# U products moved behind each head's routing, gathers begun there, and one-hot rows by pairs of tokens, in a two-block decoder kernel

## The chip, the cores and the metric

One core of one Trainium2 chip runs the whole program. The metric is device microseconds of one execution, compared as the median of several. The names are those of the profile: PE (matrix engine, with PEld for its weight loads), DVE (vector engine), ACT (scalar engine), POOL (GpSimd), SP (the queue that issues most DMAs).

## The reference, cut to what matters

The program is two decoder blocks on 512 tokens of width 1024. The change touches only its last layer, a product-key expert layer ("PEER"), which for 512 tokens, 8 heads, 2 x 128 keys and 16384 experts computes:

```
q = (h @ w_q).reshape(B, S, 8, 256)
s1 = einsum('bshd,hnd->bshn', q[..., :128], keys1);  s2 = ... keys2
v1, i1 = top_k(s1, 16);  v2, i2 = top_k(s2, 16)
cand = v1[..., :, None] + v2[..., None, :]
vals, c = top_k(cand.reshape(..., 256), 16)
expert = e1 * 128 + e2
gate = softmax(vals)
act = gelu(einsum('td,ted->te', h, u_tab[expert]))
out = x + einsum('te,ted->td', gate * act, v_tab[expert])
```

Each token thus has 8 x 16 = 128 experts; each has a row u and a row v of 1024 numbers.

## The kernel before, in words

The first some 1626 us are the rest of the network and are not touched. `peer` (L1354) then works in three stages.

**Routing.** For each of 8 heads `proj_tr` multiplies h by that head's part of w_q (48 matmuls of 512 columns; every product of this kernel is three matmuls of split fp32 halves, `mm3`), `route` (L1540) scores the keys (16 small matmuls) and finds the top 16 of 128 twice and of 64 candidates once by MAX8, FIND_INDEX8 and MATCH_REPLACE8 on DVE, then turns them into expert numbers by one-hot sums on DVE. Tiles of this stage come from the pool `p_rt` with two buffers. The softmax over all heads stands once behind the loop (L1385 to L1392), as does the number of each expert of the last 128 tokens, `ei` (L1394).

**Gates.** The first 384 tokens (DT = 3 blocks of 128) are computed densely: all 16384 experts for every token, with a gate matrix that is mostly zero. `gates` (L1500) builds that matrix, four tokens at a time, 96 times: DVE writes one-hot rows `ehot` (L1525) and their product with the gate's three bf16 parts, `p` (L1528); PE makes four 128 x 128 blocks from them with 12 matmuls (L1533); ACT copies the bank into a tile of 16 tokens (L1535), which goes to DRAM (`Gd`, L1538). Four tokens lie side by side in the last dimension of `ehot` and `p`, so each matmul reads every fourth bf16 element.

**Experts.** Experts go in 128 groups of 128. `up(e)` (L1423) loads 512 KB of U through `load_w` (ACT writes the high part, DVE subtracts for the low part, L194 and L195; three buffers each), makes 24 matmuls of 384 columns (name A) and applies Gelu. Group e's result is then multiplied by its gates (L1471), split, and multiplied by 512 KB of V: 18 matmuls of 512 columns (name acc), accumulated in six PSUM banks over all 128 groups. 42 groups (AHEAD) are made before the first V product, 12 of them spilled to DRAM; the other 86 go one per V product. The last 128 tokens are not dense: `gather(j)` (L1410) fetches for each of the 128 expert slots one row of u and v per token by an indirect DMA of POOL (1 MB), DVE makes the dot product (L1415) and adds the weighted v row into x (L1419), ACT does the Gelu between (L1417, L1418). They are spread over the V products.

**What sets the order.** Each engine runs its own instructions in the order that a list scheduler wrote at build time. The scheduler takes what its own model of the times holds to be ready, in program order where several are. `tc.high_priority` and `tc.issue_after(i)` move that order: the second keeps an instruction behind i on i's engine. A tile of a pool waits until the buffer that it takes is free.

Of the kernel before, what the change touches and what calls it, by code (L numbers as in the profile page):

```python
# [7 lines left out]
F32 = mybir.dt.float32  # L8
F32R = mybir.dt.float32r
BF = mybir.dt.bfloat16  # L10
# [7 lines left out]
NT = 4  # L18
DT = 3
TG = 16  # L20
# [162 lines left out]
class Prog:  # L183
# [5 lines left out]
    def split(s, h, l, src, eng="act"):  # L189
        nc = s.nc  # L190
        if eng == "dve":
            r = nc.vector.tensor_copy(h, src)
        else:
            r = nc.scalar.activation(h, src, AF.Copy)  # L194
        s.sub = (nc.gpsimd if eng == "pool" else nc.vector).tensor_tensor(l, src, h.bitcast(F32), ALU.subtract)  # L195
        return r
# [1157 lines left out]
    def peer(s, Y):  # L1354
# [4 lines left out]
        with ExitStack() as ctx:  # L1359
            P = lambda name, bufs, **k: ctx.enter_context(tc.tile_pool(reuse_waits="tile", name=name, bufs=bufs, **k))  # L1360
            one, two, gp = P("p_one", 1), P("p_two", 2), P("p_g", 2)
# [4 lines left out]
            nc.sync.dma_start(s.iota, a["cf"][:, 392:])  # L1366
            s.iota4 = one.tile([128, 128, 4], BF, name="iota4")
            nc.vector.tensor_copy(s.iota4, s.iota[:, :, None].to_broadcast([128, 128, 4]))

            s.E = one.tile([128, NT, 2, 128], F32, name="E")  # L1370
            s.gate = one.tile([128, NT, 8, 16], F32, name="gate")
            with tc.tile_pool(reuse_waits="tile", name="p_rt", bufs=2) as rt:
                s.rank = rt.tile([128, 16, 16 * NT], BF, name="rank", bufs=1)
# [9 lines left out]

                g = s.gate.rearrange("p i h r -> p (i h) r")
                n = 8 * NT  # L1385
                sm = rt.tile([128, n], F32, name="sm")
                nc.vector.tensor_copy(sm, g[:, :, 0])
                nc.vector.tensor_tensor(g, g, sm[:, :, None].to_broadcast([128, n, 16]), ALU.subtract)
                nc.scalar.activation(g, g, AF.Exp)
                nc.vector.tensor_reduce(sm, g, AX.X, ALU.add)  # L1390
                nc.vector.reciprocal(sm, sm)
                nc.vector.tensor_tensor(g, g, sm[:, :, None].to_broadcast([128, n, 16]), ALU.mult)  # L1392
            ei = one.tile([128, 128], I32, name="ei")
            nc.vector.scalar_tensor_tensor(ei, s.E[:, DT, 0], 128.0, s.E[:, DT, 1], op0=ALU.mult, op1=ALU.add)  # L1394
            s.Gd = s.dram.tile([NG, 128, 128, TG], F32, name="Gd")
            with tc.tile_pool(reuse_waits="tile", name="p_hot", bufs=2) as hp:
                s.gates(hp, gp)

            rows = P("p_rows", 3)
            act = two.tile([128, 128], F32, name="act")  # L1400
            wt = two.tile([128, 128], F32, name="wt")
            late = P("p_late", 1)
            x = late.tile([128, 1024], F32, name="x")
            nc.sync.dma_start(x, s.x2[:, DT, :])
            hx = late.tile([128, 1024], F32, name="hx")
            nc.sync.dma_start(hx, s.h2)
            eg = late.tile([128, 128], I32, name="eg")
            gx = s.gate[:, DT].rearrange("p h r -> p (h r)")

            def gather(j):  # L1410
                r = rows.tile([128, 2048], F32, name="r")
                nc.gpsimd.indirect_dma_start(out=r, out_offset=None, in_=a["uv"],  # L1412
                                             in_offset=bass.IndirectOffsetOnAxis(ap=eg[:, j:j + 1], axis=0))
                c = slice(j, j + 1)
                nc.vector.scalar_tensor_tensor(r[:, :1024], r[:, :1024], 1.0, hx,  # L1415
                                               op0=ALU.mult, op1=ALU.mult, accum_out=act[:, c])
                nc.scalar.activation(wt[:, c], act[:, c], AF.Gelu)  # L1417
                nc.scalar.activation(wt[:, c], wt[:, c], AF.Copy, scale=gx[:, c])  # L1418
                nc.vector.scalar_tensor_tensor(x, r[:, 1024:], wt[:, c], x, op0=ALU.mult, op1=ALU.add)  # L1419
            acc = None  # L1420
            wd = s.dram.tile([len(SPILL), 128, ND], F32, name="wd")

            def up(e):  # L1423
                with tc.high_priority(offset=U_AHEAD) if e < 6 else nullcontext():
                    U = s.load_w(a["ut"][e], 1024)
                A = s.bank("A")[:, :ND]
                for k in range(8):
                    s.mm3(A, U(128 * k, 128), (Y[0][:, k, :ND], Y[1][:, k, :ND]), k == 0, k == 7)
                if e in SPILL:
                    w = two.tile([128, ND], F32, name="ws", bufs=2)  # L1430
                else:
                    w = two.tile([128, ND], F32, name="w", bufs=UP + 1)
                    wq[e] = w
                nc.scalar.activation(w, A, AF.Gelu)
                if e in SPILL:
                    nc.sync.dma_start(wd[SPILL.index(e)], w)
            wq = {}
            ahead = AHEAD
            for e in range(ahead):
                up(e)  # L1440

            room, n = [0], ahead
            for e in range(128):
                both = e not in SPILL and n < 128
                room.append(room[-1] + (9 if both else 0 if e in SPILL else 4))
                n += both
            pace = [max(0, min(128, int(128 * (r / room[-1] - .05) / .9))) for r in room]

            gs, subs, m = {}, [], NG // 8

            def fetch(e):
                b, i = e // 8, e % 8
                if i == 0:
                    gs[b] = gp.tile([128, NG, 8, TG], F32, name="g", tag="g")
                i *= m
                nc.sync.dma_start(gs[b][:, i:i + m], s.Gd[i:i + m, :, 8 * b:8 * b + 8, :].rearrange("g p e t -> p g e t"))
            for e in range(8):
                fetch(e)
            for e in range(128):
# [3 lines left out]
                if e in SPILL:  # L1463
                    wq[e] = two.tile([128, ND], F32, name="ws", bufs=2)
# [4 lines left out]
                w3 = w.rearrange("p (g t) -> p g t", t=TG)  # L1469
                with tc.issue_after(subs[e - 2].ins) if e > 1 else nullcontext():  # L1470
# [3 lines left out]
                last = s.split(wh, wl, w)  # L1474
                subs.append(s.sub)
                V = s.load_w(a["uv"][128 * e:128 * e + 128, 1024:], 1024)
                if acc is None:
                    acc = [[s.bank("acc") for n in range(2)] for i in range(DT)]
# [21 lines left out]
    def gates(s, two, gp):  # L1500
# [3 lines left out]
        for i in range(DT):  # L1504
# [4 lines left out]
            T = two.tile([128, 5, 128], BF, name="T", bufs=DT)  # L1509
            nc.scalar.activation(T[:, :3], b[:, :384].rearrange("p (k t) -> p k t", k=3), AF.Copy)  # L1510
# [117 lines left out]
```

## Time and profile before

| | us |
|---|---|
| median of 3 runs (3015.78 to 3022.39) | 3018.95 |
| profiled execution, whole | 3021.56 |
| its span, first to last instruction | 3019.8 |

All times inside the profile are counted from the start of the span. An engine is busy while it has an instruction; matmuls overlap, so the pace of PE is read from the starts of successive matmuls and not from their durations. [...]

### The profile page before, as it was taken

How to read it: one execution, taken by the hardware profiler on the slowest of the kernel's cores; microseconds unless marked ns; L12 is line 12 of the kernel's file. 1: busy time of each engine (PE TensorE's matmuls, PEld its weight loads, DVE VectorE, ACT ScalarE, POOL GpSimd, SP SyncE). 2: the span in 40 equal slices, each digit the busy share in tenths (PEclk: the TensorE clock that was granted, in tenths of full speed). 3: DMA queues.
4: the chain of work that ended last, by engine and by line, in shares of the span. 5: the costliest groups of instructions: out<-in, count | busy, mean ns of one | idle time of the engine just before them, and what ended most of it. 6: DMA issues, size and time to landing. Idle time of an engine off the chain costs nothing. (4 is left out here: it accounts for less than half of the span.)

```text
span 3019.8 us, 44411 instructions
## 1 busy us (share of the span) xinstructions
PE 2901.3 (96%) x17102; PEld 2602.8 (86%) x17103; DVE 2012.7 (67%) x3633; ACT 1340.5 (44%) x2383; POOL 607.4 (20%) x587
## 2 busy tenths in 40 slices
PE   8999999999899999999999799997999999999998
PEld 7877878888789999999988599997888889988977
DVE  5986445553566676765345997775667788787875
ACT  5244433332455565656423345554334344444432
POOL 3001010000455555452200000000111222222210
PEclk9999999999999999999999899998999999999999
DMA  5321132223345555454763134445788899988985
GB/s 194 98 71 63 57 98 98 97 92 98 109 143 161 150 159 161 137 168 141 228 228 127 53 107 143 169 175 180 244 301 307 297 323 337 334 328 299 332 279 198
DMA packets 200149, 549.62 MB, mean 182 GB/s; under 512 B 17360, under 2 KB 90704, under 8 KB 179072
## 3 DMA queue, kind: packets, MB, share of 16 engines
q1 hardware_dynamic: 149184, 358.34, 36.0%
q0 software_dynamic: 49600, 184.76, 17.5%
q10 hardware_dynamic: 1152, 3.67, 0.4%
q8 instruction: 134, 2.20, 0.3%
q14 instruction: 79, 0.65, 0.1%
HBM read 476.52 MB, written 70.19 MB: 181 GB/s over the span
## 5 line engine op out<-in xcount | busy, mean ns | idle before, releaser
L195 DVE TENSOR_TENSOR wl<-wraw,wh 128x1024 fp32r<-128x1024 f32 x474 | 590.3, 1246 | 305.3 <-ACT wh L194 303.4
L194 ACT ACTIVATE wh<-wraw 128x1024 fp32r<-128x1024 f32 (+1 forms) x495 | 520.8, 1054 | 581.6 <-PE bank L201 126.7
L1412 POOL DMA_INDIRECT r<-in_uv_dram,eg x128 | 175.6, 1372 | 1162.7 <-ACT eg L1486 945.9
L202 PE MATMUL A<-yh,wl 128*128 128x384 f32 x1024 | 346.3, 338 | 7.5 <-DVE wl L195 7.4
L200 PE MATMUL A<-yh,wh 128*128 128x384 f32 x1024 | 345.6, 338 | 3.9 <-ACT wh L194 3.3
L201 PE MATMUL A<-yl,wh 128*128 128x384 f32 x1024 | 344.6, 336 | 0.0
L200 PE MATMUL acc<-wh 128*128 128x512 f32 x768 | 304.1, 399 | 19.4 <-ACT wh L194 19.4
L201 PE MATMUL acc<-wl,wh 128*128 128x512 f32 x768 | 305.5, 398 | 0.9 <-DVE wl L195 0.9
L202 PE MATMUL acc<-wh,wl 128*128 128x512 f32 x768 | 292.6, 397 | 3.8 <-DVE wl L195 3.8
L1415 DVE SCALAR_TENSOR_TENSOR r<-r,hx 128x1024 f32<-128x1024 f32 x128 | 156.3, 1221 | 110.1 <-DMA r<-in_uv_dram,eg 108.7
L200 PE MATMUL p<-yh,wh 128*128 128x256 f32 x736 | 214.1, 291 | 7.0 <-DVE l L195 3.8
L202 PE MATMUL p<-yh,wl 128*128 128x256 f32 x736 | 215.7, 293 | 1.4 <-DVE wl L195 1.4
L201 PE MATMUL p<-yl,wh 128*128 128x256 f32 x736 | 213.4, 290 | 0.0
L202 PEld LDWEIGHTS A<-yh,wl 128*128 128x128 f32 x1024 | 192.9, 188 | 10.6 <-DVE wl L195 10.5
L200 PEld LDWEIGHTS A<-yh,wh 128*128 128x128 f32 x1024 | 193.2, 189 | 8.5 <-ACT wh L194 4.2
L201 PEld LDWEIGHTS A<-yl,wh 128*128 128x128 f32 x1024 | 193.1, 189 | 3.7
L200 PEld LDWEIGHTS acc<-wh 128*128 128x128 f32 x768 | 146.2, 190 | 51.0 <-ACT wh L194 20.8
L201 PE MATMUL bank<-yl,wh 128*128 128x512 f32 (+1 forms) x480 | 184.1, 384 | 0.3 <-DMA yl<-od 0.3
L202 PE MATMUL bank<-yh,wl 128*128 128x512 f32 (+1 forms) x480 | 183.5, 383 | 0.0
L200 PE MATMUL bank<-yh,wh 128*128 128x512 f32 (+1 forms) x480 | 182.8, 383 | 0.1
L202 PEld LDWEIGHTS acc<-wh,wl 128*128 128x128 f32 x768 | 145.2, 189 | 39.0 <-DVE wl L195 5.1
L201 PEld LDWEIGHTS acc<-wl,wh 128*128 128x128 f32 x768 | 146.4, 191 | 33.6 <-DVE wl L195 3.2
(576 smaller groups left out, 6914.8 us busy)
## 6 DMA issues: line engine op xcount, KB each, us to landing
wraw<-in_ut_dram SPq DMA_DIRECT2D x128, 512.0 KB, 4.7
wraw<-in_uv_dram SPq DMA_DIRECT2D x128, 512.0 KB, 6.2
Gd<-g SPq DMA_DIRECT2D x24, 1024.0 KB, 4.4
g<-Gd SPq DMA_DIRECT2D x128, 192.0 KB, 7.6
wraw<-in_w_up_dram SPq DMA_DIRECT2D x44, 512.0 KB, 3.7
wraw<-in_w_sb_dram SPq DMA_DIRECT2D x24, 512.0 KB, 4.3
wraw<-in_w_down_dram SPq DMA_DIRECT2D x22, 512.0 KB, 3.8
wraw<-in_w_out_dram SPq DMA_DIRECT2D x16, 512.0 KB, 3.8
```

Source lines behind the costliest of these rows:

```text
L194: r = nc.scalar.activation(h, src, AF.Copy)
L195: s.sub = (nc.gpsimd if eng == "pool" else nc.vector).tensor_tensor(l, src, h.bitcast(F32), ALU.subtract)
L200: nc.tensor.matmul(out, lhsT=L[0], rhs=R[0], start=start, stop=False)
L201: nc.tensor.matmul(out, lhsT=L[0], rhs=R[1], start=False, stop=False)
L202: nc.tensor.matmul(out, lhsT=L[1], rhs=R[0], start=False, stop=stop)
L1412: nc.gpsimd.indirect_dma_start(out=r, out_offset=None, in_=a["uv"], in_offset=bass.IndirectOffsetOnAxis(ap=eg[:, j:j + 1], axis=0))
L1415: nc.vector.scalar_tensor_tensor(r[:, :1024], r[:, :1024], 1.0, hx, op0=ALU.mult, op1=ALU.mult, accum_out=act[:, c])
```

## The change

- Of the 128 U products 64 (instead of 42) now come before the first V product. Six stand behind the routing of each head, eleven behind the gates, and the last five (DRAIN) are kept on DVE behind the last instruction of the gates. 28 of the 64 results stay in SBUF (28 buffers instead of 31) and 36 are spilled to DRAM and fetched again (before: 12 of 42), through three buffers instead of two.
- The softmax and the expert numbers of the gathers are made inside `route`, head by head, so that 21 of the 128 gathers stand among the U products of the routing, 16 among those of the gates and 91 among the V products. A gather, its dot product and its addition are three steps apart: at step e the rows fetched at e-3 are added, those fetched at e-2 are dotted, and new ones are fetched; the DVE and ACT parts are kept behind the weight split of that step. The copies of expert numbers (L1486) go away; the loads of x and hx move up to the first head.
- `route` uses one buffer per tile instead of two; `ehot` and `p` have three buffers instead of five; the gates' 16-token tile now comes from the pool of the gathered rows, which has four buffers (before: three for gathers alone).
- One-hot rows are laid out by pairs: two tokens side by side instead of four, so each matmul reads every second bf16 element. Counts and sizes of the instructions stay.

```diff
-UP = 30
-SPILL = range(6, 42, 3)
-AHEAD = UP + len(SPILL)
+TG = 16
+
+
+AHEAD, UP, UPS, DRAIN = 64, 28, 6, 5
+SPILL = [e for e in range(AHEAD) if e > 1 and e not in {AHEAD * k // (UP - 1) for k in range(UP - 1)}]
...
-            one, two, gp = P("p_one", 1), P("p_two", 2), P("p_g", 2)
+            one, two, rows = P("p_one", 1), P("p_two", 2), P("p_rows", 4)
...
-            with tc.tile_pool(reuse_waits="tile", name="p_rt", bufs=2) as rt:
...
-                nc.vector.tensor_copy(sm, g[:, :, 0])
-                nc.vector.tensor_tensor(g, g, sm[:, :, None].to_broadcast([128, n, 16]), ALU.subtract)
-                nc.scalar.activation(g, g, AF.Exp)
-                nc.vector.tensor_reduce(sm, g, AX.X, ALU.add)
-                nc.vector.reciprocal(sm, sm)
-                nc.vector.tensor_tensor(g, g, sm[:, :, None].to_broadcast([128, n, 16]), ALU.mult)
-            ei = one.tile([128, 128], I32, name="ei")
-            nc.vector.scalar_tensor_tensor(ei, s.E[:, DT, 0], 128.0, s.E[:, DT, 1], op0=ALU.mult, op1=ALU.add)
...
-            def gather(j):
...
+            flight = []
+
+            def gathers(e, hold):
+
+                with ExitStack() as c:
+                    for i in hold:
+                        c.enter_context(tc.issue_after(i))
+                    for g in [g for g in flight if e - g[0] > 2]:
+                        j, r = g[1:]
+                        k = slice(j, j + 1)
+                        nc.scalar.activation(wt[:, k], act[:, k], AF.Gelu)
+                        nc.scalar.activation(wt[:, k], wt[:, k], AF.Copy, scale=gx[:, k])
+                        nc.vector.scalar_tensor_tensor(x, r[:, 1024:], wt[:, k], x, op0=ALU.mult, op1=ALU.add)
+                        flight.remove(g)
+                    for t, j, r in flight:
+                        if e - t == 2:
+                            nc.vector.scalar_tensor_tensor(r[:, :1024], r[:, :1024], 1.0, hx,
+                                                           op0=ALU.mult, op1=ALU.mult, accum_out=act[:, j:j + 1])
+                for j in range(pace[e], pace[e + 1]):
+                    r = rows.tile([128, 2048], F32, name="r")
+                    nc.gpsimd.indirect_dma_start(out=r, out_offset=None, in_=a["uv"],
+                                                 in_offset=bass.IndirectOffsetOnAxis(ap=eg[:, j:j + 1], axis=0))
+                    flight.append((e, j, r))
...
-            for e in range(ahead):
-                up(e)
...
+            early = [0 if e < 8 else (e - 7) // 2 if e < 8 * UPS else 4 * UPS - 4 + (e - 8 * UPS + 1) for e in range(AHEAD + 1)]
+            pace = early[:-1] + [min(128, int(early[-1] + (128 - early[-1]) * r / room[-1] / .95)) for r in room] + [128] * 3
+            e = 0
+            with tc.tile_pool(reuse_waits="tile", name="p_rt", bufs=1) as rt:
+                s.rank = rt.tile([128, 16, 16 * NT], BF, name="rank")
+                nc.scalar.activation(s.rank, s.iota[:, :16, None].to_broadcast([128, 16, 16 * NT]), AF.Copy)
+                for h in range(8):
+                    q = {}
+
+                    def ev(f, b, q=q):
+                        q[f] = rt.tile([128, 512], F32, name="q", tag=f"q{f}")
+                        nc.scalar.activation(q[f], b, AF.Copy)
+                    s.proj_tr(Y, a["w_pq"][h], ev, tag="acc", first=h == 0)
+                    s.route(rt, q, keys, h)
+                    if h == 0:
+                        nc.sync.dma_start(x, s.x2[:, DT, :])
+                        nc.sync.dma_start(hx, s.h2)
+                    while e < UPS * (h + 1):
+                        up(e)
+                        gathers(e, s.last)
+                        e += 1
+            s.Gd = s.dram.tile([NG, 128, 128, TG], F32, name="Gd")
+            with tc.tile_pool(reuse_waits="tile", name="p_hot", bufs=2) as hp:
+                last = s.gates(hp, rows)
+                while e < AHEAD:
+                    with tc.issue_after(last) if e >= AHEAD - DRAIN else nullcontext():
+                        up(e)
+                    gathers(e, s.last)
+                    e += 1
+            acc = [[s.bank("acc") for n in range(2)] for i in range(DT)]
+            gp = P("p_g", 2)
...
-                js = slice(pace[e], pace[e + 1])
-                if js.stop > js.start:
-                    with tc.issue_after(last.ins):
-                        nc.scalar.activation(eg[:, js], ei[:, js], AF.Copy)
-                for j in range(js.start, js.stop):
-                    gather(j)
+                gathers(AHEAD + e, s.last)
+            for e in range(3):
+                gathers(AHEAD + 128 + e, ())
...
-            T = two.tile([128, 5, 128], BF, name="T", bufs=DT)
-            nc.scalar.activation(T[:, :3], b[:, :384].rearrange("p (k t) -> p k t", k=3), AF.Copy)
+            E = two.tile([128, 64, 2, 2], BF, name="E", bufs=DT)
+            nc.scalar.activation(E.rearrange("p a k v -> p k a v"), b[:, :256].rearrange("p (k a v) -> p k a v", k=2, v=2), AF.Copy)
+            T = two.tile([128, 64, 3, 2], BF, name="T", bufs=DT)
...
-                st = gp.tile([128, 128, TG], F32, name="g", tag="g")
-            hot = two.tile([128, 2, 128, 4], BF, name="ehot", bufs=5)
-            nc.vector.tensor_tensor(hot, s.iota4[:, None].to_broadcast([128, 2, 128, 4]),
-                                    T[:, :2, None, :].to_broadcast([128, 2, 128, 4]), ALU.is_equal)
-            p = two.tile([128, 3, 128, 4], BF, name="p", bufs=5)
-            nc.vector.tensor_tensor(p, hot[:, None, 0].to_broadcast([128, 3, 128, 4]),
-                                    T[:, 2:, None, :].to_broadcast([128, 3, 128, 4]), ALU.mult)
+                st = gp.tile([128, 2048], F32, name="r").rearrange("p (e t) -> p e t", t=TG)
+            hot = two.tile([128, 2, 2, 128, 2], BF, name="ehot", bufs=3)
+            nc.vector.tensor_tensor(hot.rearrange("p a k e v -> p (a k) e v"), s.iota2[:, None].to_broadcast([128, 4, 128, 2]),
+                                    E.to_broadcast([128, 4, 128, 2]), ALU.is_equal)
+            p = two.tile([128, 2, 3, 128, 2], BF, name="p", bufs=3)
+            last = nc.vector.tensor_tensor(p, hot[:, :, :1].to_broadcast([128, 2, 3, 128, 2]),
+                                           T.to_broadcast([128, 6, 128, 2]).rearrange("p (a k) e v -> p a k e v", k=3), ALU.mult)
...
-                    nc.tensor.matmul(b[:, 128 * v:128 * v + 128], lhsT=hot[:, 1, :, v], rhs=p[:, k, :, v],
+                    nc.tensor.matmul(b[:, 128 * v:128 * v + 128], lhsT=hot[:, v // 2, 1, :, v % 2], rhs=p[:, v // 2, k, :, v % 2],
...
+        return last.ins
...
-            nc.vector.tensor_tensor(s.E[:, :, c, 16 * h:16 * h + 16], hh[:, 0], hh[:, 1], ALU.add)
+            nc.vector.tensor_tensor(E[:, c], hh[:, 0], hh[:, 1], ALU.add)
+        nc.vector.tensor_copy(s.E.rearrange("p i c x -> p c i x")[:, :, :, 16 * h:16 * h + 16], E[:, :, :DT])
+        nc.vector.scalar_tensor_tensor(E[:, 0, DT], E[:, 0, DT], 128.0, E[:, 1, DT], op0=ALU.mult, op1=ALU.add)
+        nc.vector.tensor_copy(s.eg[:, h, :], E[:, 0, DT])
+
+        g = s.gate[:, :, h, :]
+        nc.vector.tensor_tensor(g, vals, vals[:, :, :1].to_broadcast([128, NT, 16]), ALU.subtract)
+        nc.scalar.activation(g, g, AF.Exp)
+        sm = two.tile([128, NT], F32, name="sm", bufs=2)
+        nc.vector.tensor_reduce(sm, g, AX.X, ALU.add)
+        nc.vector.reciprocal(sm, sm)
+        nc.vector.tensor_tensor(g, g, sm[:, :, None].to_broadcast([128, NT, 16]), ALU.mult)
```

## Rows read from the trace of the kernel before

**Rows 1.** The page's busy times of the whole span.
```profile
PE 2901.3 (96%) x17102; PEld 2602.8 (86%) x17103; DVE 2012.7 (67%) x3633; ACT 1340.5 (44%) x2383; POOL 607.4 (20%) x587
```

**Rows 2.** Windows: length; busy PE, PEld, DVE, ACT, POOL (instructions); granted clock; DMA share; GB/s.
```profile
1626.00:1850.00 224.00, 199.22 (x1072) 183.03 (x1070) 204.02 (x1057) 86.33 (x115) 0.00 (x0) 0.93 0.31 99
1850.00:2088.00 238.00, 237.65 (x1734) 229.75 (x1732) 170.80 (x215) 138.26 (x146) 0.00 (x0) 1.00 0.47 166
2088.00:2105.00 17.00, 0.50 (x1) 0.50 (x2) 1.55 (x4) 1.70 (x3) 0.00 (x0) 0.56 0.83 270
2105.00:3005.00 900.00, 884.12 (x4256) 776.03 (x4255) 668.58 (x845) 363.25 (x767) 175.59 (x128) 0.99 0.85 299
...
3005.00:3019.00 14.00, 9.59 (x42) 7.44 (x40) 4.23 (x7) 0.53 (x1) 0.00 (x0) 0.98 0.28 113
```

**Rows 3.** Waits of PE, in the routing and in the gates: total, times, longest.
```profile
PE acc L202 <- DVE wl L195: 17.9, 1, 17.9
...
PE acc L200 <- ACT wh L194: 16.8, 1, 16.8
```

**Rows 4.** Timeline of PE: first product, scores, one A and one acc group.
```profile
1626.20 0.56 PE L200 MATMUL acc<-yh,wh 128*128 128x256 f32 x1
...
1645.05 1.50 PE L1550 MATMUL acc<-keys,q 128*128 128x128 f32 x12
...
2562.69 0.34 PE L200 MATMUL A<-yh,wh 128*128 128x384 f32 x1
...
2566.88 0.39 PE L200 MATMUL acc<-wh 128*128 128x512 f32 x1
...
2571.06 0.34 PE L200 MATMUL A<-yh,wh 128*128 128x384 f32 x1
```

**Rows 5.** Chain that ended last, gates: one of its pieces.
```profile
1862.00 5.66 PE acc L1533 x48
```

**Rows 6.** Timeline of PE: two matmuls of the first V product, behind the gates.
```profile
2108.93 0.63 PE L200 MATMUL acc<-wh 128*128 128x512 f32 x1
2109.36 0.63 PE L201 MATMUL acc<-wl,wh 128*128 128x512 f32 x1
```

**Rows 7.** DVE in weight splits (L195) during the routing.
```profile
1626.00:1850.00 224.00, 45.61 (x42) 0.93 0.31 99
```

**Rows 8.** Two tiles' instructions: last of a routing, one-hot rows; duration min/median/max, first and last start.
```profile
L1609 DVE TENSOR_TENSOR E<-hot x16: 203/217/239, 1686.2 to 1833.0; 128x64 f32<-128x64 bf16 x16
...
L1525 DVE TENSOR_TENSOR ehot<-iota,T x96: 678/692/696, 1840.1 to 2080.6; 128x1024 bf16<-128x1024 bf16 x96
L1528 DVE TENSOR_TENSOR p<-ehot,T x96: 947/951/955, 1845.5 to 2083.0; 128x1536 bf16<-128x1536 bf16 x96
```

**Rows 9.** DVE busy on one-hot rows (gates), then on gathered rows (experts).
```profile
1838.00:2090.00 252.00, 148.73 (x192) 1.00 0.47 164
...
2120.00:3005.00 885.00, 319.62 (x384) 1.00 0.86 303
```

**Rows 10.** Groups by form, 1640 to 2200: weight split, table load.
```profile
L195 DVE TENSOR_TENSOR wl<-wraw,wh 128x1024 fp32r<-128x1024 f32 x81 | 98.5, 1220 | 27.7 <-ACT wh L194 27.3
...
L1389 ACT ACT_TABLE_LOAD x1 | 1.3, 1283 | 0.0
```

**Rows 11.** Groups by form: bf16 matmuls that read every fourth element, and adjacent ones.
```profile
L1533 PE MATMUL acc<-p,ehot 128*128 128x128 bf16 x1152 | 142.3, 297 | 0.0
...
L506 PE MATMUL sc<-maskb,identb 128*128 128x128 bf16 x32 | 7.6, 237 | 0.0
```

**Rows 12.** Gathers: time to landing, and DVE's wait for it.
```profile
DMA to landing us min/median/max: 5.7/8.9/15.5
...
DVE r L1415 <- DMA r<-in_uv_dram,eg: 108.7, 57, 6.2
```

**Rows 13.** DMA issues: the gates' tile.
```profile
Gd<-g SPq DMA_DIRECT2D x24, 1024.0 KB, 4.4
```

**Rows 14.** Window inside the routing, where U products ran beside it.
```profile
1740.00:1850.00 110.00, 107.14 (x602) 103.89 (x601) 104.09 (x465) 49.89 (x67) 0.00 (x0) 0.98 0.38 120
```

More of the change, by code (lines that the diff above doesn't have):

```diff
@@ L1365, in peer @@
             s.iota = one.tile([128, 128], F32, name="iota")
[L1366 to L1370, printed above, removed]
+            nc.sync.dma_start(s.iota, a["cf"][:, 392:520])
+            s.iota2 = one.tile([128, 128, 2], BF, name="iota2")
+            nc.vector.tensor_copy(s.iota2, s.iota[:, :, None].to_broadcast([128, 128, 2]))
@@ new lines, in peer @@
+            wt = one.tile([128, 128], F32, name="wt")
+            x = one.tile([128, 1024], F32, name="x")
+            hx = one.tile([128, 1024], F32, name="hx")
+            flight = []
[19 more added lines that the diff above has]
+                    flight.append((e, j, r))
@@ new lines, in peer, with up @@
+            wd = s.dram.tile([len(SPILL), 128, ND], F32, name="wd")
+            wq = {}
+            def up(e):
+                with tc.high_priority(offset=U_AHEAD) if e < 6 else nullcontext():
+                    U = s.load_w(a["ut"][e], 1024)
+                A = s.bank("A")[:, :ND]
+                for k in range(8):
+                    s.mm3(A, U(128 * k, 128), (Y[0][:, k, :ND], Y[1][:, k, :ND]), k == 0, k == 7)
+                if e in SPILL:
+                    w = two.tile([128, ND], F32, name="ws", bufs=3)
+                else:
+                    w = two.tile([128, ND], F32, name="w", bufs=UP)
+                    wq[e] = w
+                nc.scalar.activation(w, A, AF.Gelu)
+                if e in SPILL:
+                    nc.sync.dma_start(wd[SPILL.index(e)], w)
@@ new lines, in peer @@
+            room, n = [0], AHEAD
+            for e in range(128):
+                both = e not in SPILL and n < 128
+                n += both
+                room.append(room[-1] + (13 if both else 5))
+            early = [0 if e < 8 else (e - 7) // 2 if e < 8 * UPS else 4 * UPS - 4 + (e - 8 * UPS + 1) for e in range(AHEAD + 1)]
[3 more added lines that the diff above has]
+                s.rank = rt.tile([128, 16, 16 * NT], BF, name="rank")
@@ L1420, in peer @@
[L1420 to L1436, printed above, removed]
@@ L1463, in peer @@
                 if e in SPILL:
-                    wq[e] = two.tile([128, ND], F32, name="ws", bufs=2)
+                    wq[e] = two.tile([128, ND], F32, name="ws", bufs=3)
                     nc.sync.dma_start(wq[e], wd[SPILL.index(e)])
@@ L1473, in peer @@
                 wl = two.tile([128, ND], F32R, name="wl")
[L1474 to L1475 removed]
+                s.split(wh, wl, w)
+                subs.append(s.last[1])
                 V = s.load_w(a["uv"][128 * e:128 * e + 128, 1024:], 1024)
[L1477 to L1478 removed]
                 for i in range(DT):
@@ L1519, in gates @@
+            g = pair(b[:, 256:384])
+            nc.scalar.activation(T[:, :, 0], g, AF.Copy)
+            r = two.tile([128, 2, 128], F32, name="r", bufs=1)
+            for k in range(2):
+                nc.vector.tensor_tensor(pair(r[:, k]), pair(r[:, 0]) if k else g, T[:, :, k], ALU.subtract)
+                nc.vector.tensor_copy(T[:, :, k + 1], pair(r[:, k]))
+            TT.append((E, T))
         for t in range(0, 128 * DT, 4):
-            T, F = TT[t // 128]
-            T = T[:, :, t % 128:t % 128 + 4]
+            a = slice(t % 128 // 2, t % 128 // 2 + 2)
@@ L1577, in route @@
             o += n * w
-        vals = s.gate[:, :, h, :]
+        vals = two.tile([128, NT, 16], F32, name="vals", bufs=2)
         cx = two.tile([128, NT, 16], I32, name="cx")
@@ L1597, in route @@
         nc.vector.tensor_tensor(R[:, 1], cx, m, ALU.subtract)
+        E = two.tile([128, 2, NT, 16], F32, name="E", bufs=2)
         for c in range(2):
```

57 lines of the change are left out of this document (12 added, 45 removed).

## The prediction, made before the changed kernel was run

> **What bounds the kernel now.** I read the page's busy times first: PE is busy for 96% of the span, DVE for 67% [rows 1]. Such a kernel gains from PE work saved, or from the few places where PE stands. So next I cut the expert layer into its stages [rows 2]: in the routing (1626 to 1850) PE is busy 199 of 224 us at a granted clock of 0.93 while DVE is busy 204; in the gates PE has no gap; between gates and experts lies a hole of 17 us; among the experts PE is busy 884 of 900 us. PE's own waits [rows 3] name the two holes: 17.9 us for the low half of a w_q weight, which DVE had not made because it was full of routing, and 16.8 us for the first V product, whose gates had still to go through DRAM.
>
> Busy time hides the pace, so I take that from starts [rows 4]. A U product, 24 matmuls, runs from 2562.69 to 2566.88: 4.19 us. A V product takes 4.18 us, 0.232 us for each 512 columns, so a head's 48 matmuls of w_q take 11.1 us; its 16 scores take about 2.0. In the gates 48 matmuls take 5.66 us [rows 5], 0.118 each, 136 us for all 1152. The work of PE is then 8 x (11.1 + 2.0) = 105, 128 x 4.19 = 536, 136, and 128 x 4.18 = 535: 1312 us. From 1626 to 3020 it had 1394. So about 82 us are lost, which is all that filling holes can give: by stage the experts lose 14 (86 x 4.19 + 535 = 895 of some 909, as PE works 9.6 us beyond 3005 [rows 2] and so to about 3015), the tail 5, the hole 17, routing and gates the remaining 46.
>
> **The change, part by part.**
>
> *U products behind the routing.* No work goes away on PE. A head now costs PE 11.1 + 2.0 + 6 x 4.19 = 38.2 us. On DVE a head's routing is at most (204.0 - 45.6) / 8 = 19.8 us by what DVE did beside weight splits [rows 2, 7]; some of that is norms, softmax and the first gates, so I take 19. New are its own softmax and index instructions: nine short ones of about 0.1 to 0.2 us (a 64-element one lasts 0.22 [rows 8]), 1.1 us. Eight weight splits of 1.2 us [rows 10] make 9.8; 21 gathers over eight heads, at 319.6 / 128 = 2.5 us of DVE each [rows 9], make 6.6. DVE: 36.5 of PE's 38.2 us. So PE sets the routing stage, barely, and DVE needs to be almost perfectly ordered. It won't be: the three weight buffers cover 3 x 4.19 = 12.6 us of PE, a routing lasts 19, and its instructions stand ahead of that head's U splits. U products did run beside routing: from 1740 to 1850 PE was busy 107 of 110 us with DVE at 104 [rows 14]. The wait per head thus lies between nothing and 19 + 1.2 - 12.6 = 7.6 us; I take 3, nearer to rows 14, since the routing's dependent instructions leave places for splits. PE then ends the routing stage at 1626 + 8 x 41.2 = 1956.
>
> ACT gets a table load at each turn between Gelu and Exp, 16 at 1.28 us [rows 10], 21 us in a stage where it is under half busy [rows 2]: nothing, unless a U split queues behind an Exp that waits for DVE; that is in the 3 us. SP has 24 more spill writes and as many reads of 192 KB, and the loads of x and hx earlier: covered, as DMA is at 31% there [rows 2]. POOL's gathers move past routing and gates, where it had nothing to do [rows 2].
>
> *Gates.* The last head's routing ends on DVE at 1626 + 7 x 41.2 + 11.1 + 2 + 1 + 19 = 1948. From the last expert sum to the first `p` took 1833.0 to 1845.5 [rows 8], 12 us, so `p` starts at 1960. DVE then has 149 us of one-hot rows [rows 9], eleven splits (13) and about twelve gathers (30), 192, of which 12 fit into the pause: 180. The gates' DVE work ends at 2140. PE has 16 U products and 1152 matmuls in that stage, 67 + 136 = 203, and comes to 1956 + 203 = 2159 if nothing else holds it.
>
> *Pairs.* Every fourth bf16 element costs: the gates' matmul lasts 297 ns where an adjacent read lasts 237 [rows 11]. With every second element the matmul's pace lies between 0.118 (no gain) and 0.066 us, what 128 columns cost if they flow like the 384 of a U product, at 4.19 / 24 = 0.175 us with some 0.012 of it fixed: up to 60 us of PE time. I take the fast end, because a step of two bf16 has the four bytes of the U product's own step. Yet it gives next to nothing, as DVE then sets the stage: 2140 plus the five drained U products, 5 x 4.19 = 21, is 2161, against PE's 2159 without any gain. [...]
>
> *DRAIN.* The hole of 17 us and the half-speed matmuls behind it (0.43 us instead of 0.232 [rows 6]) are covered by those 21 us, which sit where the gates go through DRAM. Behind the five waiting splits on DVE only gathers queue.
>
> *Experts.* PE: 64 x 4.19 + 535 = 803, plus the 14 us lost now: 817. DVE has 22 splits and 37 gathers fewer. DVE's 108.7 us of waits for rows that have not landed [rows 12] go, since a dot product now comes two steps later (8.4 us or more against a median of 8.9 us to landing); they cost PE at most the 14, so I count nothing. Bytes per us fall (49 transfers of 0.5 to 1 MB fewer against 24 spills of 0.2 MB), so DMA should not get tighter than 85%.
>
> **Sum:** 2161 + 817 + 5 of tail = 2983 of span. Around it lie 1.8 us (3021.6 for the execution), and that execution is 2.6 above the median: **2982 us** against 3018.95, 37 less, 1.2%. A measurement of this kernel can tell about 0.2%, 6 us, from no change.
>
> **The rivals.**
>
> *Everything overlaps (faster than forecast).* If splits always fit between routing instructions, PE loses only the experts' 14 and the tail: 1626 + 306 + 203 + 817 + 5 = 2957. With the pairs' gain DVE's own work is the floor: from the first split at about 1640, 8 x 20.1 + 80 splits x 1.2 + 149 + 37 x 2.5 = 498, less 19 that may fall behind the gates, then 21 + 822: 2962. So about 2958. For it: rows 14. Against: DVE would have to be 97% full for 480 us.
>
> *U splits queue behind each routing (slower).* Place: DVE, per head. If no split gets in, PE stands 7.6 us, and starts again at half speed, as it did behind the hole: 7 us at 0.43 us a matmul [rows 6], some 3.5 lost. 11 us per head, 89 instead of the 24 of the forecast: 2982 + 65 = 3047. It decides from a loss of about 7.6 us per head on, where the whole 37 are gone. For it: the 17.9 us that PE waited for just such a split [rows 3]. Against: rows 14.
>
> *The gates slow down (no change).* Their 16-token tile now shares four buffers with gathers that hold a row for three steps. A tile that finds no second buffer waits for the write to DRAM, 4.4 us [rows 13]; if a third of the 24 tiles do, and three one-hot buffers instead of five add as much elsewhere, some 35 us are lost: 3017. Against: tiles come ahead of gathers in program order, and what DVE leaves there, splits and gathers take.
>
> *Pairs break the double rate of DVE.* `ehot` takes 0.69 us for 1024 bf16 elements, an fp32 split 1.22 for as many [rows 8, 10]. At that rate both one-hot instructions cost 1.33 us more, 128 us in all: 3110. Against: a pair still fills one 32-bit word.
>
> **How the numbers follow.** Chances: forecast 0.54, full overlap 0.16, slower gates 0.11, splits behind routing 0.16, half rate 0.03. Faster by over 0.2% holds the first two, 0.70; within 0.2% the third, 0.11; slower the last two, 0.19. The forecast's own bounds, 0 to 5 us per head around 3 and 10 us in the gates, are 2958 to 3008. The range goes from 2945, below the overlap's 2958 by what my 19 us of routing may be too long (1 us per head) and a little of the experts' 14, to 3035, which takes in the slower gates and half-way cases of the next; it leaves out about 0.19.
>
> **What would show it.** Right: U products all through the routing with PE's waits for `wl` under 5 us each; the gates' matmuls at about 0.07 us with DVE near full there; no hole behind the gates and a clock of 1.00; V products starting near 2161 and taking 817 us; DVE no longer waiting for rows. Wrong: a clock below 0.95 or PE waits above 50 us in the routing; a gates stage above 200 us; waits for `r` tiles by ACT there; a first V product after 2195.

## The result, and the profile after

The changed kernel takes 2985.88 us (median of 4 runs, 2977.70 to 2990.93) against 3017.36 of the kernel before (4 runs): a ratio of 0.9895, 95% interval 0.9868 to 0.9921, 31 us less. Forecast were 2982. The profiled execution (2977.70, its span 2975.7) is the fastest of the four, so profiles are compared with profiles below, and medians with medians.

By stage, windows of the changed kernel (columns as in [rows 2]): routing, gates, the hole behind them, the first V products, the other V products, the tail.

```profile
1626.00:1960.00 334.00, 334.00 (x1902) 320.30 (x1901) 300.43 (x1200) 162.54 (x248) 21.35 (x21) 1.00 0.61 202
1960.00:2106.00 146.00, 100.83 (x1229) 85.64 (x1226) 140.89 (x191) 101.45 (x104) 11.97 (x1) 0.94 0.44 177
2106.00:2126.00 20.00, 12.70 (x60) 12.38 (x59) 7.75 (x10) 2.36 (x9) 7.20 (x5) 0.75 1.01 356
2126.00:2260.00 134.00, 111.47 (x504) 95.62 (x503) 99.89 (x128) 46.33 (x97) 35.88 (x25) 0.91 0.95 342
2260.00:2967.00 707.00, 707.00 (x3381) 617.65 (x3380) 502.35 (x635) 276.22 (x502) 87.82 (x78) 1.00 0.82 279
2967.00:2976.00 9.00, 3.50 (x16) 2.49 (x14) 3.67 (x6) 0.00 (x0) 0.00 (x0) 0.82 0.43 175
```

PE no longer stands in the routing (199 of 224 us before), and among most V products it never stands. But the gates, where it had no gap before, now leave it 45 of 146 us, and 2106 to 2260, where V products begin, another 30 of 154, with DMA at 0.95 to 1.01. PE's waits from 1626 on say for what (us in total, times, longest):

```profile
PE acc L1540 <- DVE p L1535: 34.1, 44, 1.2
PE A L200 <- ACT wh L194: 11.9, 3, 8.9
PE acc L1540 <- ACT r L1542: 9.7, 8, 1.2
PE acc L200 <- ACT wh L194: 9.1, 3, 6.5
PE A L200 <- ACT w L1419: 7.3, 1, 7.3
```

The two long waits of [rows 3] are gone; 44 short ones for one-hot rows and some for weights have come. The places of the stages stand in two tiles' instructions (columns as in [rows 8]), the last of a routing and the gates' own:

```profile
L1618 DVE TENSOR_TENSOR E<-hot x16: 218/226/243, 1665.1 to 1945.3; 128x64 f32<-128x64 bf16 x16
...
L1540 PE MATMUL acc<-p,ehot x1152: 217/218/312, 1959.3 to 2105.0; 128*128 128x128 bf16 x192
L1532 DVE TENSOR_TENSOR ehot<-iota,E x96: 680/684/694, 1950.2 to 2101.8; 128x1024 bf16<-128x1024 bf16 x96
L1535 DVE TENSOR_TENSOR p<-ehot,T x96: 946/951/957, 1954.8 to 2103.3; 128x1536 bf16<-128x1536 bf16 x96
```

The one-hot instructions last as long as before, a gates' matmul 218 ns for 297 [rows 11]. Its pace stands in the chain that ended last (start, us, what):

```profile
1959.47 2.08 PE acc L1540 x36
```

That is 0.058 us a matmul against 5.66 / 48 = 0.118 [rows 5]: over 1152 of them the pairs take 136 - 67 = 69 us off PE's 1312, leaving 1243. From 1626 to the end PE had 1350, so some 107 us are lost now, for 82 before: all that the profiled span gained (44 us) is less than what the pairs alone take off PE, and the moves opened more than they closed. Behind the gates, the first multiplication of a U result by its gates, which starts the V products (columns as in [rows 8]):

```profile
L1482 DVE TENSOR_TENSOR w<-w,g x92: 549/552/557, 2146.0 to 2954.7; 128x384 f32<-128x384 f32 x92
```

Last, POOL's timeline around the gates (start, us, what, idle before):

```profile
1898.40 0.94 POOL L1401 DMA_INDIRECT r<-in_uv_dram,eg  x1 [15.13 <-DVE hot L1615]
2094.03 14.45 POOL L1401 DMA_INDIRECT r<-in_uv_dram,eg  x1 [194.69 <-ACT r L1542]
```

The 16 gathers planned among the gates found their buffers taken by the gates' tiles: in program order the call of `gates`, with all 24 of its tiles, stands ahead of them, and both go through the same four buffers. They came from 2094 on, 29 gathers of 1 MB up to 2260.

### The profile page after: what moved, and what is told of

It reads as the page before. It is cut to its first block, busy times and chain, and to the rows that moved or that the text cites. A ratio compares the mean times of both kernels' runs of the same rounds, so it can differ in the third digit from the quotient of the medians.

```text
span 2975.7 us, 44517 instructions
## 1 busy us (share of the span) xinstructions
PE 2844.8 (96%) x17103; PEld 2546.0 (86%) x17103; DVE 2022.5 (68%) x3683; ACT 1339.8 (45%) x2311; POOL 597.3 (20%) x587
## 3 DMA queue, kind: packets, MB, share of 16 engines
q10 hardware_dynamic: 1152, 3.67, 0.4%
## 4 chain that ended last, share of the span: by engine, by line
PE 82%; DVE 7%; DMA 4%; issue 3%; POOL 2%; ACT 1%; SPq 0%; DVEq 0%; POOLq 0%; ACTq 0%
PE acc L201 7%; PE acc L202 7%; PE acc L200 7%; PE bank L200 6%; PE bank L201 6%; PE bank L202 6%; PE A L202 6%; PE A L200 6%; PE A L201 6%; PE p L200 4%; PE p L201 4%; PE p L202 4%; PE gd L996 2%; DVE ehot L1532 1%; DVE p L1535 1%
## 5 line engine op out<-in xcount | busy, mean ns | idle before, releaser
L195 DVE TENSOR_TENSOR wl<-wraw,wh 128x1024 fp32r<-128x1024 f32 x474 | 592.7, 1251 | 370.4 <-ACT wh L194 368.6
L1401 POOL DMA_INDIRECT r<-in_uv_dram,eg x128 | 164.2, 1283 | 1105.8 <-DVE x L1393 662.1
L200 PE MATMUL acc<-wh 128*128 128x512 f32 x768 | 288.7, 399 | 9.1 <-ACT wh L194 9.1
L1393 DVE SCALAR_TENSOR_TENSOR x<-r,wt,x 128x1024 f32<-128x1024 f32 x128 | 163.7, 1279 | 5.9 <-ACT wt L1392 5.9
```

The source lines that it names most:

```text
L195: s.last = r.ins, (nc.gpsimd if eng == "pool" else nc.vector).tensor_tensor(l, src, h.bitcast(F32), ALU.subtract).ins
L200: nc.tensor.matmul(out, lhsT=L[0], rhs=R[0], start=start, stop=False)
L1393: nc.vector.scalar_tensor_tensor(x, r[:, 1024:], wt[:, k], x, op0=ALU.mult, op1=ALU.add)
```

## The experiments

Each run's ratio is to the kernel before on the same chip, which took 3016.74 us there in experiments 1 (pairs alone, moves alone), 2 and 5, 3014.32 in 3, 4 and the first two of 6, 3017.30 in the rest. Where medians of two runs are subtracted below, they can come from different chips; the intervals of the ratios make such a difference uncertain by up to some 10 us.

**1. Pairs without the moves, moves without the pairs.** The kernel before with the changed `gates` layout, and the changed kernel with the layout of before:

```diff
-            hot = two.tile([128, 2, 128, 4], BF, name="ehot", bufs=5)
+            hot = two.tile([128, 2, 2, 128, 2], BF, name="ehot", bufs=5)
...
-                    nc.tensor.matmul(b[:, 128 * v:128 * v + 128], lhsT=hot[:, 1, :, v], rhs=p[:, k, :, v],
+                    nc.tensor.matmul(b[:, 128 * v:128 * v + 128], lhsT=hot[:, v // 2, 1, :, v % 2], rhs=p[:, v // 2, k, :, v % 2],
```

> The kernel of before with the pairs alone. Theory: there PE sets the gates' stage (238 us, no gap), since U products stand between the gates; with pairs the 1152 matmuls fall from 136 to 87 us and DVE's 149 + 26 splits x 1.2 = 180 us become the bound: the stage goes from 238 to 180 to 195 us and the whole to some 2970 us (ratio 0.981 to 0.988), as good as the whole change. Rival: the order of the instructions or DVE's waits keep the stage near 230 us, gain 10 us or less (ratio 0.997 to 1.0).

> The changed kernel with the one-hot rows of before (four tokens side by side), all else as changed. Theory: DVE sets the gates' stage, so pairs add nothing here: PE needs 12 x 0.118 = 1.42 us for four tokens, DVE 1.48; the stage stays near the 146 us of the changed kernel (at most 155), the whole within 10 us of it: a ratio to before of 0.987 to 0.993. Rival: the pairs carry the gain; PE sets the stage again, it takes 180 us or more and the whole comes to 3016 us or more (ratio 1.00).

Pairs alone: 2951.04 us, ratio 0.9779 (0.9753 to 0.9805), 66 us less and twice the gain of the whole change. The moves alone: 2994.11, ratio 0.993 (0.9908 to 0.9952), 23 us less; pairs on top of them bring 8 (11 by the ratios, whose intervals overlap). In the kernel before, U products fill the gates, so PE sets that stage (busy 237.65 of 238 us [rows 2]), and of the 69 us saved on it 66 are won. The gates of pairs alone, then of the moves alone, as windows:

```profile
1853.00:2027.00 174.00, 171.48 (x1737) 163.84 (x1735) 167.01 (x216) 126.60 (x144) 0.00 (x0) 1.00 0.64 225
```

```profile
1957.00:2122.00 165.00, 157.91 (x1243) 142.72 (x1242) 145.16 (x194) 110.92 (x106) 3.19 (x3) 1.00 0.42 164
```

The first is 64 us shorter than the 238 of [rows 2], with as many U products in it (585 matmuls of tile A; 582 before). In the changed order only 85 such matmuls are left among the gates, PE needs 158 us even without pairs, and below that DVE's 145 are the floor. The chain of pairs alone also has the pace by itself, where nothing but the layout differs from the 5.66 us of [rows 5]:

```profile
1908.93 2.77 PE acc L1534 x48
```

**2. No gathers planned among the gates.**

```diff
-... else 4 * UPS - 4 + (e - 8 * UPS + 1) for e in range(AHEAD + 1)]
+... else 4 * UPS - 3 for e in range(AHEAD + 1)]
```

> The changed kernel without the 16 gathers planned among the gates' U products; the 107 behind the first 21 are spread over the V products. Theory: those 16 could not start during the gates (their buffers held the gates' tiles) and came in a burst behind them, with DMA full and PE short of weights from 2106 to 2260; without them that stretch loses some 15 us less: ratio 0.982 to 0.986. Rival: the burst is not what starves PE there, or the 16 gathers cost as much later: within 5 us of the changed kernel or slower (0.988 or more).

2952.55 us, ratio 0.9783 (0.9758 to 0.9807): 33 us below the changed kernel (22 between the two profiles). Its gates end 6 us later, so the 154 us behind the last gate are compared, first of the changed kernel, then of this one:

```profile
2105.50:2259.50 154.00, 124.17 (x560) 108.08 (x561) 108.14 (x138) 48.91 (x104) 43.58 (x29) 0.89 0.96 343
2111.30:2265.30 154.00, 144.44 (x692) 127.91 (x693) 96.61 (x123) 56.53 (x100) 23.69 (x19) 0.97 0.88 303
```

PE is busy 144 us there instead of 124, at a granted clock of 0.97 instead of 0.89 (1.00 is the full clock). The changed kernel's mean holds stretches at half pace: from 2121.0 to 2125.5, behind a wait of 7.3 us, the clock was 0.50 and a matmul of A came every 0.32 us instead of 0.17. The difference in busy time places 20 of the 22 us. POOL's wait before it is as long (194.9 us), but 19 gathers come in the 166 us from its end on instead of 29. The burst was the price of gathers held back, and it was larger than I expected.

**3. A tile of its own for the gates** (`st` from two buffers of its own; 22 instead of 28 U results kept).

```diff
-                st = gp.tile([128, 2048], F32, name="r").rearrange("p (e t) -> p e t", t=TG)
+                st = two.tile([128, 128, TG], F32, name="st", bufs=2)
```

> The changed kernel with a 16-token tile of its own for the gates (two buffers) instead of one from the four row buffers; 22 instead of 28 U results stay in SBUF and 42 instead of 36 are spilled, to make room. Theory: what held the 16 gathers among the gates back was only the buffers; with them free the gathers land among the gates, the burst of DMA behind the gates and the low clock there are gone, and the 30 to 40 us come back as in the run without gathers among the gates, less what 16 gathers of 2.5 us on DVE add to a stage that DVE sets: last one-hot row 20 to 40 us later than 2103, 2960 to 2985, a ratio of 0.978 to 0.989. Rival: the gathers' DVE work costs the gates all that the burst cost the experts, and the time is that of the changed kernel (2975 to 2995, 0.987 to 0.992).

2965.39 us, ratio 0.9839 (0.9816 to 0.9862): the time that the theory gave, but not by its way. POOL's timeline:

```profile
1968.66 1.69 POOL L1401 DMA_INDIRECT r<-in_uv_dram,eg  x1 [2.83 <-DVE x L1393]
2124.43 1.68 POOL L1401 DMA_INDIRECT r<-in_uv_dram,eg  x1 [154.08 <-DVE x L1393]
```

Twelve more gathers ran ahead of the gates' first matmul (33 instead of 21), then POOL waited 154 us again, now for DVE's additions, which came only behind the one-hot rows: the gates have no room for gathers on DVE either (busy 142.7 of the 143 us from 1981 on). The gates' matmuls began at 1981.6 instead of 1959.3, and the burst was smaller (17 gathers from 2126 to 2260 for 24, DMA still at 0.97). How much of the 20 us is due to the buffers and how much to the place of the twelve stays open, as does the part of the six results more that were spilled.

**4. All gathers among the V products.**

```diff
-            early = [0 if e < 8 else (e - 7) // 2 if e < 8 * UPS else 4 * UPS - 4 + (e - 8 * UPS + 1) for e in range(AHEAD + 1)]
+            early = [0] * (AHEAD + 1)
```

> The changed kernel with all 128 gathers among the V products, none in routing or gates: this takes back the part of the change that begins gathers with the routing. Theory: the 21 early gathers cost nothing and bring little, since DVE has room among the V products and PE is the bound there; routing and gates end as in the changed kernel (last one-hot row at about 2100), the burst of gathers behind the gates is gone, DMA among the V products rises by 21 MB and stays below 0.95: 2950 to 2970, a ratio of 0.978 to 0.985, like the run without gathers among the gates. Rival: early gathers are needed, as 128 gathers do not fit beside the V products; DMA or DVE sets the end, PE waits there, and the time is 2985 or more, a ratio of 0.99 or more.

2971.84 us, ratio 0.9859 (0.9834 to 0.9884), just above the theory's range, 19 us slower than experiment 2, from which it differs by the 21 gathers of the routing alone. PE's waits from 2260 on, none in experiment 2:

```profile
PE acc L200 <- ACT wh L194: 15.5, 10, 3.1
```

DMA's share is 0.92 in 2500 to 2700 and in 2700 to 2900, where experiment 2 has 0.84 and 0.89. So gathers in the routing are worth about 1 us each (19 us / 21): they take 21 MB out of the stage where weights begin to come late (the 15.5 us above). That they "cost nothing and bring little" was wrong in its second half.

**5. DRAIN 0**: the last five U products are no longer kept behind the gates.

```diff
-AHEAD, UP, UPS, DRAIN = 64, 28, 6, 5
+AHEAD, UP, UPS, DRAIN = 64, 28, 6, 0
```

> The changed kernel with no U product held back behind the gates (DRAIN 0). Theory: PE has nothing to do while the gates go through DRAM; a hole of 17 us or more at a low clock stands behind the gates, 15 to 20 us more in all: ratio 0.994 to 0.998. Rival: the five U products fill PE's gaps inside the gates instead, or products of the V stage move up: within 5 us of the changed kernel (0.988 to 0.991).

2979.36 us, ratio 0.9877 (0.9856 to 0.9898): not slower. PE's waits show a hole longer than that of [rows 3]:

```profile
PE acc L200 <- ACT wh L194: 49.1, 4, 36.8
```

But the products now run among the gates. The matmuls of tile A there (length; busy PE, count; clock, DMA share, GB/s), changed kernel and DRAIN 0:

```profile
1960.00:2106.00 146.00, 16.08 (x85) 0.94 0.44 177
1964.00:2125.00 161.00, 45.74 (x248) 0.94 0.53 201
```

That is 6.8 products more, the five and some two others. Moved from one idle place of PE to another, they are worth nothing; my theory of 15 to 20 us fell, the rival held, with a time 1.5 us beyond its 5.

**6. U products among the gates.** Experiment 2 with 80 U products ahead, one written in after each 16-token tile:

```diff
-AHEAD, UP, UPS, DRAIN = 64, 28, 6, 5
+AHEAD, UP, UPS, DRAIN = 80, 28, 6, 5
...
+                def between():
+                    if step[0] < AHEAD - DRAIN:
+                        up(step[0])
+                        gathers(step[0], s.last)
+                        step[0] += 1
-                last = s.gates(hp, rows)
+                last = s.gates(hp, rows, between)
...
+            if t % 16 == 12:
+                between()
```

> The changed kernel with no gathers planned among the gates, and with 80 instead of 64 U products ahead of the first V product, one of them written into the gates after every second tile of eight four-token steps' half (after each 16 tokens), the last five still kept behind the gates. Theory: in the gates DVE needs 149 us for the one-hot rows plus 1.2 us for each weight split among them, and PE 87 us for the 1152 matmuls plus 4.19 us for each U product, so PE has room there for some 15 to 20 products that cost DVE 18 to 24 us; each product that PE makes in its own gaps saves 4.19 us later for 1.2 now. PE should be over 95 % busy in 1960 to 2120 (69 % in the changed kernel), the first V product should come some 20 us later than 2147, and the 16 products fewer among the V products give 67 us: a total of 2915 to 2935, a ratio of 0.967 to 0.973. Rival: the V products then have no U products to hide their weights behind, and since each V product moves more bytes per us (V weights, fetched U results and gathered rows) DMA sets the expert stage: its share there above 0.95, PE with gaps, and 2950 or more, a ratio of 0.978 or more.

The same with 76, and with seven more gathers in the routing:

```diff
-AHEAD, UP, UPS, DRAIN = 80, 28, 6, 5
+AHEAD, UP, UPS, DRAIN = 76, 28, 6, 5
...
-... (e - 7) // 2 if e < 8 * UPS else 4 * UPS - 3 for e in range(AHEAD + 1)]
+... (e - 7) * 7 // 10 if e < 8 * UPS else (8 * UPS - 7) * 7 // 10 for e in range(AHEAD + 1)]
```

> As the run with 80 products ahead, but with 76, and with 28 of the 128 gathers among the U products of the routing instead of 21 (0.7 per product instead of 0.5), none among the gates. Theory: the same gain from PE's gaps in the gates, four products less of it (2915 to 2940, a ratio of 0.967 to 0.974), and since DVE is 90 % busy in the routing the seven gathers more (2.5 us each, 17 us) still fit there, with PE not waiting above 10 us. Rival: DVE is the bound of the routing by then, so the routing ends up to 15 us later than 1948 and the total is 2940 or more; if DMA among the V products is the bound, this kernel with fewer gathers left there is faster than the one with 80.

With 90, spread evenly over the gates:

```diff
-AHEAD, UP, UPS, DRAIN = 80, 28, 6, 5
+AHEAD, UP, UPS, DRAIN = 90, 28, 6, 5
...
-                    if step[0] < AHEAD - DRAIN:
+                    tiles[0] += 1
+                    while step[0] < 8 * UPS + (AHEAD - DRAIN - 8 * UPS) * tiles[0] // 24:
```

> As the kernel with 80 U products ahead and pairs, but with 90, 37 of them written evenly into the gates. Theory: with 80 PE had run out of U products by 2080 and stood 20 of the last 60 us of the gates; ten more fill that at 1.2 us of DVE each, which lengthens the gates by 12 and takes 42 off the V products: 2923.05 less 10 to 20 us, 2903 to 2913, a ratio of 0.963 to 0.967. Rival: the V products are by now set by DMA (0.95 in 2260 to 2500), ten U products fewer among them leave the same bytes and ten more spills and fetches, and nothing is won: 2920 to 2935, a ratio of 0.968 to 0.974.

And the 80, then experiment 2, with the four-token layout (the diff of experiment 1 the other way round):

> The kernel with 80 U products ahead, many of them among the gates and no gathers there, with the four-token layout. Theory: here PE has 24 U products for the time that the pairs free, as the kernel before had 42 products for its routing and gates, so PE's 49 us of gate matmuls reach the end nearly whole: 2923.05 plus 35 to 50 us, so 2958 to 2973, a ratio of 0.981 to 0.986; PE busy in all of the gates, without waits for one-hot rows of more than 10 us in all. Rival: the pairs are worth some 10 us wherever the gates stand, and what they gave alone comes from something else in the kernel before: 2930 to 2940, a ratio of 0.972 to 0.976.

> The changed kernel with no gathers planned among the gates and with the four-token one-hot layout of the kernel before. Theory: in this order of the work the pairs shorten PE's work in a stage that DVE sets (149 us of one-hot rows in a stage of 146 us), so their 49 us of PE time turn into PE waits and almost nothing of them reaches the end, whether or not gathers burst behind the gates: 2952.55 plus 8 to 20 us, so 2960 to 2973, a ratio of 0.982 to 0.986. Rival: it was the burst of gathers that swallowed the pairs' gain, and without it they are worth their 49 us, or the 66 that they gave alone: 3000 or more, a ratio of 0.994 or more.

| | median us | ratio (95%) |
|---|---|---|
| 80 ahead, pairs | 2923.05 | 0.9699 (0.9676 to 0.9722) |
| 76 ahead, 28 gathers in the routing | 2929.60 | 0.9724 (0.9700 to 0.9748) |
| 90 ahead | 2924.07 | 0.9700 (0.9684 to 0.9716) |
| 80 ahead, four-token layout | 2971.15 | 0.9842 (0.9824 to 0.9860) |
| experiment 2, four-token layout | 2967.60 | 0.9841 (0.9825 to 0.9856) |

With 80 the kernel is 63 us below the changed one and beats the pairs alone too. With 76 the theory held too, with the gates' first matmul at 1966.1 instead of 1961.6 for the seven gathers. The gates with 80, and with 90 the gates and most V products, as windows:

```profile
1961.00:2080.00 119.00, 119.00 (x1117) 115.86 (x1116) 103.24 (x132) 77.78 (x92) 0.00 (x0) 1.00 0.60 218
2080.00:2141.00 61.00, 41.93 (x516) 35.39 (x514) 59.96 (x81) 43.62 (x44) 12.63 (x1) 0.89 0.42 173
```

```profile
1959.00:2140.00 181.00, 181.00 (x1707) 176.29 (x1706) 157.71 (x199) 119.33 (x141) 0.00 (x0) 1.00 0.62 221
2260.00:2900.00 640.00, 620.78 (x2833) 525.17 (x2832) 508.11 (x663) 254.39 (x487) 133.44 (x94) 0.99 0.90 324
```

With 80, PE is full to 2080 and then out of products (92% busy in 1960 to 2120, where I had said over 95); with 90 it is full to 2140, as the theory said, but the V products then leave PE 19 of 640 us, and their waits for weights are longer (19.8 us in 1950 to 2900, against 7.4 with 80). The rival held: nothing is won in the sum. That DMA is what makes these weights late is not shown, as its share there is 0.90 with 90 and 0.89 with 80 (2260 to 2910). The two layouts in four orders of the work (medians, us):

| order | four-token | pairs | pairs' worth |
|---|---|---|---|
| kernel before | 3016.74 | 2951.04 | 66 |
| changed kernel | 2994.11 | 2985.88 | 8 |
| without gathers among the gates | 2967.60 | 2952.55 | 15 |
| the same, 80 ahead | 2971.15 | 2923.05 | 48 |

By the ratios, which take the chips into account, the last column is 66, 11, 18 and 43. The pairs' gain on PE is nearly the same in all rows (69 us at a granted clock of 1.00, less where some groups of 12 run at half the pace, as at 2073.9 of the changed kernel, 1.46 us against 2.08 / 3 = 0.69; the median of a gates' matmul is 218 ns in every run with pairs and 297 in every run without). What reaches the end is set by whether PE has U products to make in its place, and the burst is not what swallowed it: without it (row three) 15 to 18 us reach the end. Without pairs, products among the gates are worth nothing (2967.60, 2971.15), as PE is nearly full there without them (158 of 165 us in experiment 1).

## Why the prediction was right, and where it was not

The total fell 4 us from the forecast, but by steps that missed on both sides; that it came so near is luck.

**Routing: right place, wrong content.** I put the last routing at 1948, it ended at 1945.3. But the 24 us of PE waits did not come: PE was busy all the 334 us. The first scores of two heads (start, us, what), and all scores (columns as in [rows 8]):

```profile
1825.59 0.61 PE L1558 MATMUL acc<-keys,q 128*128 128x128 f32 x4
1863.32 0.61 PE L1558 MATMUL acc<-keys,q 128*128 128x128 f32 x4
...
L1558 PE MATMUL acc<-keys,q x128: 271/275/275, 1635.6 to 1905.2; 128*128 128x128 f32 x128
```

A head took 37.7 us, as in the sum without waits (38.2), and the last scores came at 1905, some 22 us earlier than forecast. The last routing then took 40 us on DVE from there to its expert sum, not 20, with ten weight splits (12 us) beside it; the two misses cancel. PE filled the time: up to 1948 it made 1279 matmuls of tile A, 53.3 products instead of the 48 written there, and 5.3 x 4.19 = 22 us. The steps that failed are the wait of 3 us per head, which was nothing as splits got in beside the routing (the condition of the rival of full overlap), and "PE then ends the routing stage": I took the written order of U products for the executed one.

**Gates: too long by 35 us.** They began as forecast (first `p` 1954.8, said 1960; first matmul 1959.3) and ended at 2105 instead of 2140. The one-hot rows ran from 1950.2 to 2104.3, 154 us with the pauses of the first ones, near the 149 [rows 9] that I used. From the first `p` on the stage lasted 149 us on DVE where I had 180. The eleven splits (13 us) and twelve gathers (30) were the mis-sized terms: three splits and no gather ran there, as the products had gone ahead and the gathers were held. By the same error PE, for which I had 16 products there, five of them drained, had 85 / 24 = 3.5 before the drained ones.

**Pairs: right about the pace, wrong as a judgement.** I took 0.066 us for 0.118; it is 0.058. The fixed 0.012 us in it was an estimate that no row or run shows: the 0.175 us for 384 columns and 0.232 for 512 that I had read leave nearly none, and 0.060 for 128. Nor is it shown that the four bytes of the step are what counts, by which I chose the fast end; shown is that 48 matmuls went from 5.66 us to 2.77 (experiment 1). That the faster pace gives "next to nothing, as DVE then sets the stage" held within the change (8 us, experiment 1), yet I read it as a property of the pairs. It was one of the moves, which had emptied the gates of PE work; by [rows 2] alone, PE full and DVE at 171 of 238, the pairs had up to 67 us to give, and gave 66.

**DRAIN: a cover with gaps, and not needed.** The first V product was to start at 2161, the multiplication by its gates started at 2146.0. The hole was not covered: PE was busy 28 of the 41 us from the last gate on (2105 to 2146), at a mean granted clock of 0.84. Experiment 5 shows that the drained products are as good among the gates.

**Experts: 817 + 5 forecast, 2975.7 - 2146.0 = 830 measured.** DVE's 108.7 us of waits for rows [rows 12] are gone, as said. "DMA should not get tighter than 85%" failed where V products begin, with 0.95 and more up to 2260; behind that it was 0.82. (The transfers fewer that I weighed there are 22 + 37 = 59, not 49.) The rival with the shared four buffers named the right place, but the wrong victim: the gates did not wait for a tile, the gathers waited for the gates, and the price, 33 us by experiment 2, fell on the V products behind. The signs I gave for it ("waits for `r` tiles by ACT") looked at the wrong queue; POOL's was the one.

The sum: V start 15 early, experts 8 late, so a span 7 below the forecast's 2983. The forecast put the median 0.8 below the span, and it lies 10 above the span of the profiled execution: that the two nearly cancel is luck as well.

## What to carry to other kernels

Before moving work, write for each stage what every engine would need there, and leave movable work in the stage where that engine is otherwise light: 16 more U products among the gates, where DVE sets the pace (busy 141 of 146 us in the changed kernel), took 30 us off with pairs, and nothing without them, where PE was full (158 of 165 us). What an instruction's speed-up is worth depended on the order around it (66, 8, 15 and 48 us for the pairs in four orders), so when a change combines both, try the speed-up in the old order too. The gathers that shared their buffers with the gates were not spread by being planned into that stage: POOL waited 194.7 us, and 29 came as a burst in the 166 us from 2094 on, where DMA was at 0.95 and more behind the gates and PE waited 21 us for weights. Buffers of their own did not spread them either (154 us of wait in experiment 3), as their work on DVE had no room there.

## What the runs showed of the hardware that I had not expected

A bf16 matmul of 128 columns whose operands are read at every second element comes every 0.058 us, one at every fourth every 0.118, twice as long, while the duration of one shrinks only from 297 to 218 ns: with these matmuls, which overlap, the pace tells what such a read costs. Both paces are at a granted clock of 1.00 (gates before, and pairs alone). The weight load shrank with it, from 117 to 97 ns. Both operands changed together, so which of the two costs is not shown. DVE, writing the same rows by pairs instead of fours, kept its 0.69 and 0.95 us [rows 8]. The rival of half rate fell; that the 32-bit word which I held against it is the reason is not shown.
